# A gMLP mixer on 1024 tokens at a time: split weights shared by two blocks, a seven-product output projection, LN1 in two VectorE passes

## The chip, the core and the metric

One core of a Trainium2 chip runs the kernel alone. The metric is the device time of one execution in microseconds (us). TensorE multiplies matrices, VectorE and ScalarE do elementwise work, GpSimd does elementwise work out of SBUF, and SyncE issues every transfer of this kernel but two.

## The reference

The kernel computes one decoder layer for x of 2048 tokens by 1024 features, all in float32, with a conditioning vector c:

```python
sh1, sc1, g1, sh2, sc2, g2 = split(silu(c) @ mod_w + mod_b, 6)
h = x * (1 + sc1) + sh1
u, v = split(gelu(h @ w_in + b_in), 2)            # 1024 features each
v = layer_norm(v)                                 # gain and bias of the mixer
sv = tril(w_s) applied over chunks of 128 tokens, per group of 128 features, + b_s
y = (u * sv) @ w_out
x = layer_norm(2**0.25 * x + (1 + g1) * y) * ln1_g + ln1_b
h = x * (1 + sc2) + sh2
y = (silu(h @ w_g) * (h @ w_u)) @ w_d             # hidden width 2816
x = layer_norm(2**0.25 * x + (1 + g2) * y) * ln2_g + ln2_b
```

## The kernel before

Each float32 operand of a matmul is split into a high and a low part in fp32r: `parts` (L91) makes the high part by a cast on ScalarE (L94) and the rest by a subtraction on VectorE (L95). A product of two operands is three matmuls, high by high, high by low and low by high (`HL`, L103). A "unit" tile holds both parts of 128 by 512.

The mixer runs over four blocks b of 512 tokens, one after the other. For a block, `v_part` computes v token-major: eight feature slices d, for each of which x is scaled and split and a row of wv is loaded and split, then 24 matmuls of 128 by 512 into eight banks of PSUM. `us_part` computes u feature-major, eight tiles i of 24 matmuls, and the spatial tiles s, four float32 matmuls each. The product u times sv is split again into yT. `y_part` multiplies yT by wo, eight slices of 24 matmuls into eight banks. So wv, wu and wo are loaded and split once for each block, four times in all. The residual, LN1 and its statistics follow during the next block's v: multiply by g1 and add alpha x on VectorE (L380, L381), statistics on VectorE, the normalisation on ScalarE (L174), gain and bias on GpSimd (L386, L388; for the last block the bias on VectorE). `h2_part` transposes the rows on TensorE (L409), scales them and writes operands for the feed-forward part to DRAM ("hop"). The feed-forward part (`ffn_in`, tiles f_0 to f_10 for each half of the tokens, and `ffn_out`) uses seven products of half-sized blocks in place of eight; its input weights are combined on GpSimd (L86).

The modulation vectors are built on the way: `mod_col` loads 512 KB of mod_w and reduces it on VectorE (L124). `spread` writes such a vector to DRAM and loads it back for all partitions (L147, L149). `ahead(makers, depth)` makes an operand that many steps before it is used. A planner puts each engine's instructions into one order before the run: among those that it takes to be ready, the one that stands first in the program; each engine and SyncE's queue then keep to that order. Tiles of one tag share a fixed number of buffers: the first block's loads share 17 buffers of 512 KB (`first`), later weight loads share three (`raw`), split weights seven units (`w`).

Of the kernel before, what the change touches and what calls it, by code (L numbers as in the profile page):

```python
# [13 lines left out]
P = 128  # L14
D = 1024
# [22 lines left out]
def gmlp_swiglu_layer(  # L38
    ctx: ExitStack,
    tc: tile.TileContext,  # L40
    x, xT, c, modwT, modb,
# [78 lines left out]
    def mod_col(k, d, plus, tag="late"):  # L120
# [91 lines left out]
    def token_major(operands, nk, name, between=()):  # L212

        ps = [[bank(f"{name}_ps{t}{h}") for h in range(2)] for t in range(NT)]
        for k, (a, w) in enumerate(operands):
            for t in range(NT):
                for part, wpart in HL:
                    for h in range(2):
                        nc.tensor.matmul(  # L219
                            ps[t][h],  # L220
                            lhsT=a[:, part, t * P : (t + 1) * P],
                            rhs=w[h][:, wpart, :],
                            start=(k == 0 and part == 0 and wpart == 0),
                            stop=(k == nk - 1 and part == 1),
                        )
            for f in between[k :: nk]:
                f()
        return ps

    def feature_major(w, rhs, name):  # L230

        ps = bank(name)
        n = 0
        for d in range(ND):
            for wpart, part in HL:
                nc.tensor.matmul(  # L236
                    ps,
                    lhsT=w[d // 4][:, wpart, (d % 4) * P : (d % 4 + 1) * P],
                    rhs=rhs[d][:, part, :],
                    start=(n == 0),  # L240
                    stop=(n == 3 * ND - 1),
                )
                n += 1
        return ps

# [5 lines left out]
    def start():  # L251
        cact = new("cact", "cact")
# [32 lines left out]
    def v_operands(b, hT):  # L285
        def operands(d):
            if b == 0:
                sh1[d] = mod_col(0, d, 0.0, "first")
                sc1[d] = mod_col(1, d, 1.0, "first")
            r = new("xh" if b else "first", f"xT{b}_{d}", HALF)  # L290
            nc.sync.dma_start(out=r, in_=xT[d, :, b * TB : (b + 1) * TB])
            nc.vector.tensor_scalar(r, r, sc1[d], sh1[d], ALU.mult, ALU.add)
            hT.append(parts(r, f"hT{b}_{d}", "hT"))
            return hT[d], load_w(wv[d * P : (d + 1) * P, :], f"wv{b}_{d}", "raw" if b else "first")

        return ahead([lambda d=d: operands(d) for d in range(ND)])

    def v_part(b, operands, between):
        ps = token_major(operands, ND, f"v{b}", between)
        if b == 0:  # L300
            env["first"].close()
            env["mix"] = phase("left", yT=(8, UNIT), raw=(3, ROW), bcv=(3, ROW), vrow=(4, ROW))
            env["bv"] = bcast(bv, "bv_bc", "bcv")
        vh = [new("vrow", f"v{b}_{t}") for t in range(NT)]
        for t in range(NT):
            for h in range(2):
                sl = slice(h * 512, (h + 1) * 512)
                nc.vector.tensor_tensor(out=vh[t][:, sl], in0=ps[t][h], in1=env["bv"][:, sl], op=ALU.add)
            nc.scalar.activation(vh[t], vh[t], AF.Gelu)

        def norm(t):
            st = stats_tile(f"lnv{b}_{t}")
# [6 lines left out]
    def us_part(b, hT, vh, norm, between, mods):
        u = [None] * ND  # L320
        yT = [None] * ND

        weights = ahead([lambda i=i: load_w(wu[i], f"wu{b}_{i}") for i in range(ND)], 1)
        if b == 0:
            setup_spatial()

        def u_tile(i):
            w = next(weights)
            p = feature_major(w, hT, f"u{b}_{i}_ps")
            u[i] = new("u", f"u{b}_{i}")  # L330
            nc.scalar.activation(u[i], p, AF.Gelu, bias=colc[:, i : i + 1])

        def s_tile(i):
            p = bank(f"s{b}_{i}_ps")
# [14 lines left out]
            nc.vector.tensor_tensor(out=sv, in0=sv, in1=u[i], op=ALU.mult)  # L349
            yT[i] = parts(sv, f"yT{b}_{i}", "yT")  # L350

        for i, step in enumerate("u0 n0 u1 n1 u2 n2 n3 u3 h u4 s0 s1 u5 s2 s3 u6 s4 s5 s6 u7 s7".split()):
            if i < len(mods):
                mods[i]()
            if step == "h":
                between()
            else:
                {"u": u_tile, "n": norm, "s": s_tile}[step[0]](int(step[1]))
        return yT

    def y_part(b, yT, following, between):
        operands = ahead([lambda i=i: (yT[i], load_w(wo[i * P : (i + 1) * P, :], f"wo{b}_{i}")) for i in range(ND)])
        ps = token_major(operands, ND, f"y{b}", between)
        following()
        rows = [new("late", f"r{b}_{t}") for t in range(NT)]
        last = b == NB - 1
        for r, p in zip(rows, ps):
            for q, sl in enumerate((lo, hi)):
                if last:
                    nc.vector.tensor_tensor(out=r[:, sl], in0=p[q], in1=env["g1"][:, sl], op=ALU.mult)  # L370
                else:
                    nc.scalar.copy(out=r[:, sl], in_=p[q])

        def norm(t):
            r = rows[t]
            xt = new("h3" if last else "late", f"x{b}_{t}")
# [452 lines left out]
```

## Time and profile before

| what | value |
|---|---|
| median of 3 runs | 1888.29 us (1886.86 to 1888.87) |
| profiled execution, its own time | 1890.18 us |
| span of the trace of that execution | 1888.5 us |
| mean granted TensorE clock, as a share of full | 0.991 |
| TensorE busy, share of the span | 98% |
| VectorE, ScalarE, GpSimd busy | 68%, 39%, 32% |
| moved by DMA | 338.72 MB |

The span runs from the first to the last instruction; the execution's own time has 1.7 us around it. Matmuls are pipelined, so a busy TensorE has no idle time between instructions but need not be at its best; what it does without a pause is read from the spacing of matmuls. The mixer's stretch is from 0 to 606 us, where the first matmul of f_0 begins.

### The profile page before, as it was taken

The numbers are of one execution on the slowest core, as the hardware profiler recorded it, in microseconds if no ns is written. First come the engines' busy times: TensorE is split into PE (matmuls) and PEld (weight loads), VectorE is DVE, ScalarE is ACT, GpSimd is POOL, SyncE is SP. The second block draws the span as 40 slices with busy tenths as digits, with TensorE's granted clock in tenths as the row PEclk, the third lists the DMA queues.
The fourth block names the chain that finished last, engine by engine and source line by source line (L and its number), as shares of the span: only waits on it lengthen the run. The fifth ranks groups of instructions, "written<-read, shape, count | busy, mean of one in ns | idle before, by whom it ended". The sixth has DMA issues, their size and how long they took to land.

```text
span 1888.5 us, 23484 instructions
## 1 busy us (share of the span) xinstructions
PE 1844.8 (98%) x8264; PEld 1528.4 (81%) x8264; DVE 1278.1 (68%) x1901; ACT 736.3 (39%) x1216; POOL 595.1 (32%) x379
## 2 busy tenths in 40 slices
PE   7999999999999899999999999999999999999997
PEld 6887888878888788888887888888888888888886
DVE  8486965875856975567768856677666344455858
ACT  3433453453454444343335433333334333333320
POOL 0000500550502565665454644554453000000104
PEclk9899999999999999999999999999999999999999
DMA  9358545564435455445645435455545656556532
GB/s 354 126 199 279 195 151 205 191 232 166 136 144 184 173 178 176 143 162 190 205 168 192 141 119 173 151 173 196 199 157 189 217 185 195 185 162 194 172 118 100
DMA packets 149320, 338.72 MB, mean 179 GB/s; under 512 B 18225, under 2 KB 22353, under 8 KB 149202
## 3 DMA queue, kind: packets, MB, share of 16 engines
q1 hardware_dynamic: 149138, 337.19, 52.9%
q8 instruction: 64, 1.05, 0.2%
q14 instruction: 54, 0.44, 0.1%
q0 software_dynamic: 64, 0.03, 0.0%
HBM read 245.14 MB, written 92.02 MB: 179 GB/s over the span
## 4 chain that ended last, share of the span: by engine, by line
PE 85%; DVE 10%; DMA 3%; issue 1%; ACT 1%; SPq 0%; DVEq 0%; ACTq 0%
PE o L597 21%; PE u_ps L236 7%; PE y_ps L219 7%; PE v_ps L219 5%; DVE modw L124 2%; PE f_5u_X L455 1%; PE f_4u_X L455 1%; PE f_3u_X L455 1%; PE f_2u_X L455 1%; PE f_9g_X L455 1%; PE f_9u_X L455 1%; PE f_8u_X L455 1%; PE f_7u_X L455 1%; PE f_7g_X L455 1%; PE f_6u_X L455 1%; PE f_6g_X L455 1%
## 5 line engine op out<-in xcount | busy, mean ns | idle before, releaser
L597 PE MATMUL o<-wd_w,alw 128*128 128x512 f32 x1848 | 419.2, 389 | 0.0
L597 PEld LDWEIGHTS o<-wd_w,alw 128*128 128x128 f32 x1848 | 346.8, 188 | 72.0
L219 PE MATMUL v_ps<-wv,hT 128*128 128x512 f32 x768 | 180.5, 397 | 16.0 <-ACT wv L94 11.9
L219 PEld LDWEIGHTS v_ps<-wv,hT 128*128 128x128 f32 x768 | 147.5, 192 | 48.1 <-ACT wv L94 12.1
L236 PE MATMUL u_ps<-hT,wu 128*128 128x512 f32 x768 | 183.2, 398 | 0.8 <-ACT h L410 0.5
L219 PE MATMUL y_ps<-wo,yT 128*128 128x512 f32 x768 | 177.6, 393 | 4.2 <-DVE sv L342 4.2
L219 PEld LDWEIGHTS y_ps<-wo,yT 128*128 128x128 f32 x768 | 145.4, 190 | 34.8 <-issue 4.5
L236 PEld LDWEIGHTS u_ps<-hT,wu 128*128 128x128 f32 x768 | 145.9, 192 | 31.8 <-issue 1.0
L95 DVE TENSOR_TENSOR alw<-al,alw 128x512 fp32r<-128x512 f32 x154 | 100.5, 687 | 87.6 <-ACT alw L94 87.6
L94 ACT CAST alw<-al 128x512 fp32r<-128x512 f32 x154 | 89.0, 620 | 140.8 <-PE o L597 138.7
L188 POOL TENSOR_TENSOR ln_rss<-ln_ves,mhalf 128x4 f32<-128x4 f32 x3 | 7.4, 2467 | 378.2 <-DVE ln_ves L187 378.2
L162 POOL TENSOR_TENSOR ln_rs<-ln_ve,mhalf 128x1 f32<-128x1 f32 x20 | 19.4, 979 | 327.1 <-DVE ln_ve L160 316.8
L95 DVE TENSOR_TENSOR wd_w<-wdl,wd_w 128x512 fp32r<-128x512 f32 x77 | 53.0, 691 | 68.5 <-ACT wd_w L94 68.5
L95 DVE TENSOR_TENSOR wu<-wu_raw,wu 128x512 fp32r<-128x512 f32 x64 | 63.4, 1004 | 51.9 <-ACT wu L94 51.8
L94 ACT CAST wd_w<-wdl 128x512 fp32r<-128x512 f32 x77 | 47.7, 622 | 106.6 <-PE o L597 78.2
L94 ACT CAST wv<-wv_raw 128x512 fp32r<-128x512 f32 x64 | 37.5, 620 | 99.5 <-PE v_ps L219 44.6
L124 DVE SCALAR_TENSOR_TENSOR modw<-modw,cact 128x1024 f32<-128x1024 f32 x48 | 58.6, 1225 | 18.9 <-DMA modw<-in_modwT 18.9
L95 DVE TENSOR_TENSOR wv<-wv_raw,wv 128x512 fp32r<-128x512 f32 x64 | 47.8, 767 | 21.8 <-ACT wv L94 21.7
L95 DVE TENSOR_TENSOR wo<-wo_raw,wo 128x512 fp32r<-128x512 f32 x64 | 47.4, 749 | 21.2 <-ACT wo L94 21.2
L94 ACT CAST wo<-wo_raw 128x512 fp32r<-128x512 f32 x64 | 38.6, 616 | 44.2 <-PE y_ps L219 43.1
L94 ACT CAST wu<-wu_raw 128x512 fp32r<-128x512 f32 x64 | 38.3, 615 | 36.3 <-PE v_ps L219 19.2
L551 DVE TENSOR_TENSOR wd<-wd,g_bc 128x512 f32<-128x512 f32 x44 | 36.9, 861 | 12.7 <-DMA wd<-in_wd 12.3
(610 smaller groups left out, 3753.4 us busy)
## 6 DMA issues: line engine op xcount, KB each, us to landing
al<-aop SPq DMA_DIRECT2D x154, 256.0 KB, 2.8
modw<-in_modwT SPq DMA_DIRECT2D x48, 512.0 KB, 8.3
aop<-aop_s SPq DMA_DIRECT2D x88, 256.0 KB, 2.0
wv_raw<-in_wv SPq DMA_DIRECT2D x32, 512.0 KB, 4.7
wu_raw<-in_wu SPq DMA_DIRECT2D x32, 512.0 KB, 4.1
wo_raw<-in_wo SPq DMA_DIRECT2D x32, 512.0 KB, 3.5
wd<-in_wd SPq DMA_DIRECT2D x44, 256.0 KB, 4.1
wdT<-wd SPq DMA_DIRECT2D x44, 256.0 KB, 4.1
```

Of the source, the lines that this page charges most:

```text
L94: nc.scalar.copy(out=o[:, 0, :], in_=src)
L95: nc.vector.tensor_tensor(out=o[:, 1, :], in0=src, in1=o[:, 0, :].bitcast(F32), op=ALU.subtract)
L124: nc.vector.scalar_tensor_tensor(out=w, in0=w, scalar=1.0, in1=env["cact"], op0=ALU.mult, op1=ALU.mult, accum_out=modc[:, j : j + 1],)
L162: nc.gpsimd.tensor_tensor(out=rs, in0=ve, in1=mhalf, op=ALU.pow)
L188: nc.gpsimd.tensor_tensor(out=rs, in0=ve, in1=mhalf.broadcast_to([P, m]), op=ALU.pow)
L219: nc.tensor.matmul(ps[t][h], lhsT=a[:, part, t * P : (t + 1) * P], rhs=w[h][:, wpart, :], start=(k == 0 and part == 0 and wpart == 0), sto ...
L236: nc.tensor.matmul(ps, lhsT=w[d // 4][:, wpart, (d % 4) * P : (d % 4 + 1) * P], rhs=rhs[d][:, part, :], start=(n == 0), stop=(n == 3 * ND ...
L455: nc.tensor.matmul(ps, lhsT=w[:, wpart, k * P : (k + 1) * P], rhs=a[k][:, part, :], start=(first and k == 0 and wpart == 0 and part == 0), ...
L551: nc.vector.tensor_tensor(out=b, in0=b, in1=env["g2"][:, cs], op=ALU.mult)
L597: nc.tensor.matmul(ps[:, cs], lhsT=a[:, part, p * P : (p + 1) * P], rhs=w[:, wpart, cs], start=(first and part == 0 and wpart == 0), stop= ...
```

## The change

The mixer runs over two pairs of blocks, 1024 tokens each, in a function `mixer(sb, jobs, u_done)` that replaces `v_part`, `us_part` and `y_part`; `load_w`, `token_major` and `feature_major` go.

- v: two passes y over its 512-column halves. In the first, x for 1024 tokens is loaded, scaled on ScalarE and split into 2 units for each slice; wv is loaded by halves and split once for the pair. u: each split tile of wu serves both blocks.
- y: u times sv stays in float32 as A. Products 1, 2, 6, 5, 7, 3, 4 of four slices each take sums of A made on VectorE and split on the way (`left_y`), and operands of wo that are loaded already split from DRAM (`right_y`).
- `wo_prep(k)`, four times in the first pair during u: loads two rows of wo, multiplies by g1, makes seven operands, splits each and stores both parts to DRAM, 512 KB each.
- LN1: alpha x is added as a bank is read; gain and bias are two `scalar_tensor_tensor` passes over 1024 columns on VectorE; nothing of it is on GpSimd but one small power for four rows. The first block's runs after product 3, the second's (`norm(1)`) in the next v or in f_0.
- The loads of x and of the raw weights share three buffers (`xs`), split weights six units (`w`). Rows of x1 are loaded back from DRAM for the transposes of all four blocks (before: of the last); two blocks' transposes lie in the second pair's u, two in ffn_in. Preparation of wd starts at f_7 (before: f_6).

```diff
+    def wo_prep(k):
...
+        def store(n, src):
+            nc.sync.dma_start(out=wot[n][k], in_=parts(src, f"wo{n}_{k}", "w").bitcast(F32))
+        def scale(q):
+            nc.vector.tensor_tensor(out=w[q], in0=w[q], in1=env["g1"], op=ALU.mult)
+            for n, cs in ((("B11", lo),), (("B21", lo), ("B22", hi)))[q]:
+                store(n, w[q][:, cs])
+        def totals():
+            b11, b12, b21, b22 = w[0][:, lo], w[0][:, hi], w[1][:, lo], w[1][:, hi]
+            for n, o, a, b in (("T1", b11, b12, b11), ("T3", b12, b22, b12), ("T2", b22, b22, b11), ("T4", b21, b21, b22)):
+                nc.vector.tensor_tensor(out=o, in0=a, in1=b, op=ALU.subtract)
+                store(n, o)
...
+    def mixer(sb, jobs, u_done):
...
+            r = new("xs", f"xT{sb}_{d}")
+            nc.sync.dma_start(out=r, in_=xT[d, :, sb * D : (sb + 1) * D])
+            nc.scalar.activation(r, r, AF.Identity, bias=sh1[d], scale=sc1[d])
+            for x, cs in enumerate((lo, hi)):
+                h[x][d] = parts(r[:, cs], f"h{blocks[x]}_{d}", ("hA", "hB")[x])
...
+            for k in range(ND):
+                w = next(made)
+                for x in range(2):
+                    for t in range(NT):
+                        for part, wpart in HL:
+                            nc.tensor.matmul(
+                                ps[x][t], lhsT=h[x][k][:, part, t * P : (t + 1) * P], rhs=w[:, wpart, :],
...
+        for i in range(ND):
+            w = next(made)
+            for x in range(2):
+                u_tile(x, i, w)
+            also("u", i)
...
+        def left_y(pr, k):
+            a11, a12, a21, a22 = (A[x, y, k] for x in range(2) for y in range(2))
+            t = s1[k // 2][:, (k % 2) * 512 : (k % 2 + 1) * 512]
+            if pr == 6:
+                for o, a, b, op in ((t, a21, a22, ALU.add), (a21, a11, a21, ALU.subtract), (a11, t, a11, ALU.subtract), (a12, a12, a11, ALU.subtract)):
+                    nc.vector.tensor_tensor(out=o, in0=a, in1=b, op=op)
+            return parts({1: a11, 2: a12, 6: a11, 5: t, 7: a21, 3: a12, 4: a22}[pr], f"y{sb}_S{pr}{k}", "hB")
...
+        def evacuate(pr, j, ps):
+            if pr in (1, 6, 7, 4):
+                x, y = {1: (0, 0), 6: (0, 1), 7: (1, 1), 4: (1, 0)}[pr]
+                with_x(x, j, (lo, hi)[y], ps[j])
+            if pr in (2, 3):
+                o = rows[0][j][:, (lo, hi)[pr == 3]]
+                add(o, ps[j], o)
+            if pr == 7:
+                o = rows[1][j][:, hi]
+                add(o, z[j], o)
+            for p, x, y in ((2, 0, 0), (3, 0, 1), (7, 1, 1), (4, 1, 0)):
+                if p == pr:
+                    bn(rows[x][j], sts[x][j], y)
+        def norm(x):
+            for t, (mu, rs, nm) in enumerate(norms_of(sts[x], f"ln1_{blocks[x]}")):
+                r = rows[x][t]
+                nc.vector.scalar_tensor_tensor(out=r, in0=r, scalar=mu, in1=env["ln1g"], op0=ALU.subtract, op1=ALU.mult)
+                nc.vector.scalar_tensor_tensor(out=r, in0=r, scalar=rs, in1=env["ln1b"], op0=ALU.mult, op1=ALU.add)
+                nc.sync.dma_start(out=x1d[blocks[x]][t * P : (t + 1) * P, :], in_=r)
...
+            for k in range(NK):
+                a, w = next(made)
+                for j in range(4):
+                    for part, wpart in HL:
+                        nc.tensor.matmul(
+                            ps[j], lhsT=a[:, part, j * P : (j + 1) * P], rhs=w[:, wpart, :],
...
+            for j in range(4):
+                evacuate(pr, j, ps)
+            if pr == 3:
+                norm(0)
+        return lambda: norm(1)
...
-    late = phase("left", late=(12, ROW))
-    mix = phase("left", w=(7, UNIT), cact=(1, ROW))
-    env["first"] = phase("left", first=(17, ROW))
-    early = phase("right", hT=(8, UNIT), u=(5, HALF), xh=(2, HALF), sv=(2, HALF))
+    late = phase("left", lc=(2, ROW), late=(10, ROW))
+    mix = phase("left", hB=(8, UNIT), u=(16, HALF), w=(6, UNIT), xs=(3, ROW), lt=(3, ROW))
+    early = phase("right", hA=(8, UNIT), sv=(2, HALF), bc=(4, ROW))
...
+    for k in range(NK):
+        jobs["u", k + 1] = [wo_prep(k)]
...
+    norm = mixer(0, jobs, lambda: None)
+    jobs = {("v", 0, 0): [norm]}
```

## Rows read from the trace of the kernel before

**Rows 1.** The page, part 1: busy time, share of the span, instructions.
```profile
PE 1844.8 (98%) x8264; PEld 1528.4 (81%) x8264; DVE 1278.1 (68%) x1901; ACT 736.3 (39%) x1216; POOL 595.1 (32%) x379
```

**Rows 2.** The page, part 5: TensorE's groups of the mixer.
```profile
L219 PE MATMUL v_ps<-wv,hT 128*128 128x512 f32 x768 | 180.5, 397 | 16.0 <-ACT wv L94 11.9
...
L236 PE MATMUL u_ps<-hT,wu 128*128 128x512 f32 x768 | 183.2, 398 | 0.8 <-ACT h L410 0.5
L219 PE MATMUL y_ps<-wo,yT 128*128 128x512 f32 x768 | 177.6, 393 | 4.2 <-DVE sv L342 4.2
```

**Rows 3.** Chain that ended last: start us, us, engine, tile, line, count.
```profile
465.08 43.52 PE v_ps L219 x192
...
272.19 0.89 PE s_ps L337 x8
```

**Rows 4.** Timeline of TensorE: start us, us, instruction, count, idle before it.
```profile
11.86 46.34 PE L219 MATMUL v_ps<-wv,hT 128*128 128x512 f32 x192 [11.86 <-ACT wv L94]
...
163.14 1.07 PE L219 MATMUL v_ps<-wv,hT 128*128 128x512 f32 x4
...
179.06 34.96 PE L219 MATMUL v_ps<-wv,hT 128*128 128x512 f32 x142 [3.90 <-DVE wv L95]
213.86 21.93 PE L236 MATMUL u_ps<-hT,wu 128*128 128x512 f32 x96
...
272.83 43.78 PE L219 MATMUL y_ps<-wo,yT 128*128 128x512 f32 x192
...
360.35 22.03 PE L236 MATMUL u_ps<-hT,wu 128*128 128x512 f32 x96 [0.22 <-DVE v L308]
...
414.59 3.27 PE L219 MATMUL y_ps<-wo,yT 128*128 128x512 f32 x13
422.05 43.03 PE L219 MATMUL y_ps<-wo,yT 128*128 128x512 f32 x179 [4.19 <-DVE sv L342]
...
645.82 0.73 PE L455 MATMUL f_1g_Y<-h2A,f_1g_w 128*128 128x512 f32 x2 [1.30 <-ACT f_1g_w L94]
647.45 2.57 PE L455 MATMUL f_1g_Y<-h2A,f_1g_w 128*128 128x512 f32 x10 [0.90 <-DVE f_1g_w L95]
...
653.53 2.58 PE L455 MATMUL f_1u_Y<-h2A,f_1u_w 128*128 128x512 f32 x10 [3.06 <-DVE f_1u_w L95]
```

**Rows 5.** SyncE's waits from 0 to 720 us: total, times, longest.
```profile
SPq L149 <- DMA g_bc_line<-modc: 17.9, 2, 9.2
```

**Rows 6.** Groups of VectorE and ScalarE by shape, 0 to 612 us.
```profile
L292 DVE TENSOR_SCALAR xT<-xT,modc 128x512 f32<-128x512 f32 x32 | 17.3, 547 | 13.6 <-DMA xT<-in_xT 13.0
...
L381 DVE SCALAR_TENSOR_TENSOR r<-x,r 128x1024 f32<-128x1024 f32 x12 | 14.5, 1222 | 0.0
...
L94 ACT CAST hT<-xT 128x512 fp32r<-128x512 f32 x32 | 19.4, 620 | 21.6 <-DVE xT L292 21.3
...
L174 ACT ACTIVATE r<-r,ln_nm,ln_rs 128x1024 f32<-128x1024 f32 x12 | 14.1, 1234 | 3.4 <-DVE ln_nm L173 3.4
```

**Rows 7.** The chain again, VectorE back to back in block 1.
```profile
164.51 2.29 DVE modw L124 x4
...
180.64 1.80 DVE wv L95 x3
```

**Rows 8.** Timeline of VectorE with GpSimd busy, two stretches.
```profile
411.48 1.77 DVE L95 TENSOR_TENSOR wo<-wo_raw,wo 128x512 fp32r<-128x512 f32 x1
...
647.32 3.41 DVE L388 TENSOR_TENSOR r<-r,ln1b_bc 128x1024 f32<-128x1024 f32 x1
```

**Rows 9.** The page, part 5: the power of four columns on GpSimd.
```profile
L188 POOL TENSOR_TENSOR ln_rss<-ln_ves,mhalf 128x4 f32<-128x4 f32 x3 | 7.4, 2467 | 378.2 <-DVE ln_ves L187 378.2
```

**Rows 10.** Windows: busy of each engine (count), granted clock, DMA share, GB/s.
```profile
20.00:40.00 20.00, 20.00 (x90) 16.57 (x89) 19.85 (x43) 7.09 (x13) 0.00 (x0) 1.00 1.03 413
...
160.00:180.00 20.00, 15.87 (x67) 12.55 (x66) 18.05 (x34) 6.76 (x13) 0.00 (x0) 0.94 1.03 419
```

**Rows 11.** DMA issues: count, KB each, median us from issue to landing.
```profile
x1d<-r SPq DMA_DIRECT2D x16, 512.0 KB, 4.9
```

More of the change, by code (lines that the diff above doesn't have):

```diff
@@ L210, in ahead @@
         return results()
[L212 to L244, printed above, removed]
     x1d = [dram.tile([TB, D], F32, name=f"x1d{b}") for b in range(NB)]
@@ L283, in setup_spatial @@
         env["wm"], env["tb"] = wm, tb
[L285 to L312, printed above, removed]
-            for q in range(2):
-                bn(vh[t], st, q)
-            normalise(vh[t], st, f"lnv{b}_{t}")
-        return vh, norm
@@ L319, in us_part @@
[L319 to L334, printed above, removed]
+    wot = {n: [dram.tile([P, 2, 512], F32, name=f"wo{n}_{k}") for k in range(NK)] for n in B_OF.values()}
@@ L348, in s_tile @@
             )
[L349 to L376, printed above, removed]
-            row = b * TB + t * P
-            nc.sync.dma_start(out=xt, in_=x[row : row + P, :])
-            if not last:
-                nc.vector.tensor_tensor(out=r, in0=r, in1=env["g1"], op=ALU.mult)
-            nc.vector.scalar_tensor_tensor(out=r, in0=xt, scalar=ALPHA, in1=r, op0=ALU.mult, op1=ALU.add)
-            st = stats_tile(f"ln1_{b}_{t}")
-            for q in range(2):
-                bn(r, st, q)
-            normalise(r, st, f"ln1_{b}_{t}")
-            nc.gpsimd.tensor_tensor(out=r, in0=r, in1=env["ln1g"], op=ALU.mult)
-            e = nc.vector if last else nc.gpsimd
-            e.tensor_tensor(out=r, in0=r, in1=env["ln1b"], op=ALU.add)
-            nc.sync.dma_start(out=x1d[b][t * P : (t + 1) * P, :], in_=r)
-        return rows, norm
@@ new lines, in s_tile @@
+            nc.vector.tensor_tensor(out=u[x, i], in0=sv, in1=u[x, i], op=ALU.mult)
+        made = ahead([lambda i=i: wu_pieces(i) for i in range(ND)], 1)
+        norm_v(0)
+        norm_v(1)
+        spatial = {3: (0, 1), 4: (2,), 5: (3, 4), 6: (5,), 7: (6, 7)}
+        for i in range(ND):
+            w = next(made)
+            for x in range(2):
+                u_tile(x, i, w)
+            also("u", i)
+            for f in spatial.get(i, ()):
+                for x in range(2):
+                    s_tile(x, f)
@@ new lines, in right_y, with with_x @@
+        def right_y(pr, k):
+            w = new("w", f"y{sb}_T{pr}{k}")
+            nc.sync.dma_start(out=w.bitcast(F32), in_=wot[B_OF[pr]][k])
+            return w
+        rows = [[new("late", f"r{b}_{t}") for t in range(NT)] for b in blocks]
+        sts = [[stats_tile(f"ln1_{b}_{t}") for t in range(NT)] for b in blocks]
+        def with_x(x, t, cs, ps):
+            xt = new("lt", f"x{blocks[x]}_{t}{cs.start}", HALF)
+            row = blocks[x] * TB + t * P
+            nc.sync.dma_start(out=xt, in_=inp_x[row : row + P, cs])
+            nc.vector.scalar_tensor_tensor(out=rows[x][t][:, cs], in0=xt, scalar=ALPHA, in1=ps, op0=ALU.mult, op1=ALU.add)
```

183 lines of the change are left out of this document (121 added, 62 removed).

## Prediction

> **What bounds the kernel now.** I read the page's busy shares first: TensorE is busy for 98% of the span, VectorE for 68% [rows 1]. The groups of the mixer come next: v, u and y have 768 matmuls of 128 by 512 each [rows 2]. A mean of 390 to 398 ns there is the life of one pipelined matmul; what one costs is its spacing, and the chain shows that: 192 of them follow each other in 43.52 us, 0.2267 us each, and a pair of spatial accumulations, one s tile, takes 0.89 us [rows 3]. So a stage without a pause is priced by its count, and what a block takes beyond that is waiting.
>
> The timeline of TensorE then says where it waits [rows 4]. The first matmul starts at 11.86 us. Block 0's v needs 46.34 us (2.8 over). Block 1's v lasts from 163.14 to 213.86, 50.7 us, 7.2 over: 3.90 us of it is a wait for VectorE's part of wv, and the 142 matmuls behind that wait take 34.96 us instead of 32.2, since the granted clock fell. Block 1's u and s last 59.0 us (213.86 to 272.83), block 2's only 54.2 (360.35 to 414.59), so 4.8 over. Block 2's y lasts from 414.59 to 465.08, 50.5 us, 7.0 over, with a wait of 4.19 us for its last operand. In f_1 three waits of 1.30, 0.90 and 3.06 us make 5.3. Blocks 2 and 3 have v and y stages without any loss. So TensorE sets the end, and the mixer's losses are hand-overs at which VectorE's queue is behind.
>
> **What the change removes from TensorE.** v and u keep 768 matmuls each. y falls from 768 to 2 pairs x 7 products x 4 slices x 4 tiles x 3 = 672. That is 96 x 0.2267 = 21.8 us, on the engine that sets the end. Spatial tiles and transposes keep their number; two blocks' transposes move to ffn_in, which changes no sum.
>
> **What else it removes.** Block 1's loss of 7.2 us in v had its cause in the queue: SyncE waited 9.2 us at a time for the round trip of the g1 vector [rows 5], the loads of the next vectors and of wv stood behind it, and VectorE then took the vectors first. In the new order that round trip falls into the first pair's u, where several operands are made ahead: -7.2. The wait for the last operand of y in block 2 came from a product u times sv that had to be made and split after the last s tile; products 1 and 2 now take the first four slices: -7.0. The extra of block 1's u goes for the larger part: -3.3 of 4.8, as transposes remain. The 5.3 us in f_1 I drop here and count its successor below. Together -22.8.
>
> **What it adds, in order of time.**
> The start. The first slice of x has 1024 columns and goes through ScalarE, 1.23 us where VectorE took 0.55 for 512, and one more cast of 0.62 stands before that of wv [rows 6]: +1.3.
>
> Block pair 0's first v pass has the same bytes as block 0's v, but x and wv have 3 buffers in place of a share of 17. A slice of x holds its buffer until VectorE has split both halves, so the second piece of wv is requested at about 13.4 us and stands behind ten loads of mod_w that found buffers. These and what is before them are some 7.4 MB, 19 to 20 us at the 413 GB/s of a full window [rows 10]; the second piece is ready near 21.4 us where TensorE wants it at 18.7. +2.7 (0 if those loads wait, 12 if more go ahead).
>
> wo_prep in u of pair 0. Back to back, a subtraction of 512 columns takes VectorE 0.60 us and a pass over 1024 columns 1.14 [rows 7]. One wo_prep is two passes and eleven operations of 512, 8.9 us; four are 35.5. In the same four steps of u (4 x 10.9, with six s tiles 48.9 us) VectorE splits wu (4.8) and reads the s tiles (7.6): 47.9 of 48.9, full, but one step of wu is always made ahead. The DMA carries 4 x (1.05 + 3.67 + 0.52) = 21 MB, 50.5 us at the 413 to 419 GB/s of the two fullest windows [rows 10]. That is 1.6 over, I take +2 (0 to 25, below).
>
> The y stages. Of 76.2 us (336 x 0.2267) VectorE needs 88 operations x 0.60 = 53 and one LN1 of about 10: 63, so it keeps pace on the whole. Behind product 7 it reads two banks and makes statistics for each tile before product 3 may write into z: the fourth is released 4.6 us after product 7 where TensorE wants it at 2.0. Other tiles can go first. +1.25 each (0 to 2.6): +2.5.
>
> The end of y in pair 0, to v. This is the weak place. After product 3 VectorE reads four banks (free at 2.8 us), makes LN1's small numbers with a power on GpSimd of 2.5 us [rows 9], at 6.6, and then does eight passes of 1.14, to 15.7. Product 4 lasts 48 x 0.2267 = 10.9, so its banks are read from 5.4 us after its end, one every 1.2 us. TensorE meanwhile can do the first block's half of the pieces that are split (2.7 us each, into the four banks of z). Two pieces are, made in VectorE's spare time in products 5 and 3, and cover just this. Then norm(1) takes VectorE for another 13 us, of which 2.5 are free for one more piece; the fifth piece is split 26.2 us after y, wanted at 22.4. +3.8, and with a clock loss as after the 3.90 us wait [rows 4], 3 us, it is +7 (0 to 15). Queued behind norm(1) on VectorE are the splits of v's pieces; TensorE waits for those.
>
> The end of y in pair 1, to f_0. The same queue, but now S1 and the weights of f_0 stand behind it: the third product of f_0 starts 2 to 3 us late, and the weights of its fourth, emitted after norm(1), come about 5 late. +8 (0 to 16), in the place of f_1's 5.3.
>
> LN1 itself costs nothing more on VectorE than the multiply and the add it replaces, two passes of 1.22 us then and now [rows 6]. Its time is covered where y and v give VectorE spare time; where the cover is gone its price is in the last two terms. The reloading of rows of x1 and the later preparation of wd cost nothing: they have tens of us until used.
>
> Added: 1.3 + 2.7 + 2 + 2.5 + 7 + 8 = 23.5. The sum: -21.8 - 22.8 + 23.5 = -21.1. Against the profiled execution's own 1890.18 us that is 1869.1; the median of the runs is 1.9 lower, so I forecast 1867 us: the matmuls' saving, with old waits exchanged for new ones.
>
> **A rule weighed against a row.** Beside GpSimd a split of 512 columns took 1.77 us and a pass of 1024 columns 3.41 [rows 8], against 0.60 and 1.14 without. Moving LN1's passes off GpSimd takes this away from the mixer, and I counted it in the waits that go. But norm(1) of pair 1 falls into f_0, where GpSimd combines weights. If each of its eight passes met it, it would last 8 x 2.2 = 17.5 us longer. The Trainium skill (SBUF — State Buffer, "Who interferes with whom") says that an instruction of VectorE with two SBUF inputs contends with one of GpSimd that reads SBUF, and that the later one is blocked for the whole instruction. By that rule the new passes, which have two SBUF inputs each, are as exposed as the additions were, and the trace agrees for those with 3.41 us.
>
> **The rivals.**
> 1. Both hand-overs and the y stages are hidden: VectorE's spare time reaches for more pieces than I count, or TensorE finds other tiles. Speaking for it: blocks 2 and 3 have no loss in v although LN1 lies there. 1867 - 17.5 = 1849.
> 2. The hand-overs cost their full price: TensorE waits until the last bank is read (9.7 us) and for norm(1) (13) less two pieces (10.9), with a clock loss 15 in each place: 1867 + 15 = 1882. For it: block 1's v, where vectors and residual passes starved the split of wv in just this way.
> 3. norm(1) in f_0 meets GpSimd in every pass: 1867 + 17.5 = 1884, no difference. Against it: GpSimd is not always busy there.
> 4. Slower: wo_prep starves u. Its 28 splits go through the six units of `w`, of which wu holds four; a split holds its unit for a cast, a subtraction and a store of 512 KB, 0.62 + 0.69 + 4.9 [rows 6, 11] = 6.2 us. Through two units that is 87 us, where 48.9 and one step ahead of 10.9 are there: 27 us of waiting in place of my 2, 1892. It decides from 23 us of waiting, that is at 5.9 us for each split. Against it: a finished step of u gives two more units, and the median store of 4.9 us holds queueing.
> That the count does not fall is no case: the loops of y are written out in the diff.
>
> **Chances.** The forecast 0.50 (its own range 1857 to 1877), rival 1 0.13, rival 2 0.15, rival 3 0.05, rival 4 0.15, the rest, between 2 and 4, 0.02. A measurement of this kernel tells about 0.2% from no change, 3.8 us. Faster takes the forecast, rival 1, and most of 2, a little of 3: 0.75. Same: 0.08. Slower: rival 4 and a little of the rest: 0.17. The range of 8 in 10 goes from rival 1's 1849 to 1889, which leaves out most of rival 4 and the outer tail of rival 1.
>
> **What the profile after would show.** 672 matmuls in y, and y stages of 76 to 79 us. The first matmul near 13.2 us and the first pass of v ending near 60. In pair 0's u, waits of TensorE for wu of 2 us or less; 20 or more would be rival 4. Behind y of both pairs, VectorE in the two LN1 passes while TensorE waits for its splits or banks. No waits like those of block 1's v and block 2's y. Wrong I would be if the planner put norm's passes after the splits (rival 1), or if stores of wo held up the loads of wu.

## Result and the profile after

The change made the kernel slower: 1945.66 us median of 4 runs (1944.42 to 1947.14) against 1887.78 (4 runs), a ratio of 1.0307 (1.0289 to 1.0325). The forecast was 1867 us, faster. The profiled execution spans 1943.9 us, 55.4 more than before.

The page's parts 1 and 5 after the change, to be held against [rows 1, 2]:

```profile
PE 1839.9 (95%) x8168; PEld 1518.1 (78%) x8168; DVE 1231.7 (63%) x1785; ACT 685.3 (35%) x1116; POOL 508.4 (26%) x327
...
L449 PE MATMUL y<-y_T,y_S 128*128 128x512 f32 x672 | 156.7, 395 | 30.6 <-ACT y_S L94 26.3
```

The 96 matmuls are gone, and every engine has less to do. But TensorE, busy 98% before, is busy 95%: the time went into waiting. The timeline of TensorE, to be read as [rows 4], says where:

```profile
12.10 7.20 PE L313 MATMUL v_ps<-wv,h 128*128 128x512 f32 x24 [12.10 <-ACT h L94]
32.03 7.47 PE L313 MATMUL v_ps<-wv,h 128*128 128x512 f32 x24 [12.74 <-ACT wv L94]
41.42 12.80 PE L313 MATMUL v_ps<-wv,h 128*128 128x512 f32 x48 [1.91 <-ACT wv L94]
55.41 11.18 PE L313 MATMUL v_ps<-wv,h 128*128 128x512 f32 x48 [1.19 <-ACT wv L94]
69.60 56.28 PE L313 MATMUL v_ps<-wv,h 128*128 128x512 f32 x240 [3.01 <-ACT wv L94]
125.72 0.62 PE L347 MATMUL u_ps<-h,wu 128*128 128x512 f32 x2
...
318.27 46.00 PE L313 MATMUL v_ps<-wv,h 128*128 128x512 f32 x202
368.26 44.06 PE L313 MATMUL v_ps<-wv,h 128*128 128x512 f32 x182 [4.00 <-DVE v L83]
...
524.79 22.03 PE L449 MATMUL y<-y_T,y_S 128*128 128x512 f32 x96
573.13 35.43 PE L449 MATMUL y<-y_T,y_S 128*128 128x512 f32 x144 [26.31 <-ACT y_S L94]
610.38 22.04 PE L449 MATMUL y<-y_T,y_S 128*128 128x512 f32 x96 [1.81 <-DVE r L83]
633.13 0.73 PE L522 MATMUL f_0g_X<-h2A,f_0g_w 128*128 128x512 f32 x2 [0.71 <-ACT f_0g_w L94]
639.51 4.14 PE L522 MATMUL f_0g_X<-h2A,f_0g_w 128*128 128x512 f32 x10 [4.09 <-DVE f_0g_w L95]
659.73 1.65 PE L522 MATMUL f_0g_Z<-h2S,f_0g_w 128*128 128x512 f32 x3 [6.06 <-DVE h2S L95]
```

Three places hold the loss: v of the first pair, 113.6 us where its 384 matmuls need 87.05; one wait of 26.31 us in y of the second pair; and f_0. By stages of the two timelines:

| stretch | before | after | difference |
|---|---|---|---|
| first matmul | 11.86 | 12.10 | +0.2 |
| v of all blocks | 184.5 | 207.5 | +23.0 |
| u, s and transposes | 228.9 | 225.7 | -3.2 |
| y of all blocks | 181.2 | 187.8 | +6.6 |
| f_0 and f_1 | 74.2 | 96.4 | +22.2 |
| the rest | | | +6.6 |

The rest is the stretch from f_2 to the end. It holds 24 of the 32 transposes of the one block whose transposes moved to ffn_in (ffn_in has 64 now, 32 before; eight take 0.79 us), a longer wait in f_10 (4.88 us, 3.16 before), and a lower clock behind that wait (the next 12 matmuls took 5.23 us, 3.04 before).

**What SyncE did in the first v.** Its timeline (start, us, transfer, count; transfers are issued in this order):

```profile
5.17 9.73 SPq L118 DMA_DIRECT2D modw<-in_modwT  x8
15.74 0.33 SPq L136 DMA_DIRECT2D bv_bc<-in_bv  x1
16.98 2.87 SPq L118 DMA_DIRECT2D modw<-in_modwT  x3
20.73 0.33 SPq L224 DMA_DIRECT2D wm<-in_ws  x1
22.02 0.33 SPq L296 DMA_DIRECT2D wv_raw<-in_wv  x1
23.27 0.33 SPq L136 DMA_DIRECT2D ln1g_bc<-in_ln1g  x1
24.51 0.33 SPq L136 DMA_DIRECT2D ln1b_bc<-in_ln1b  x1
...
54.30 0.39 SPq L142 DMA_DIRECT2D g_bc_line<-modc  x1
```

The second piece of wv is asked for at 22.02 us, behind eleven vectors of mod_w, bv and wm; ln1g and ln1b, first used at 305.5 us, go ahead of the third. At 54.30 comes the g1 row, 1024 numbers stored four bytes at a time. The windows of the two stretches:

```profile
12.00:40.00 28.00, 14.67 (x48) 11.25 (x48) 24.32 (x52) 5.97 (x9) 1.68 (x1) 0.76 1.03 417
40.00:70.00 30.00, 24.38 (x98) 19.31 (x99) 17.18 (x36) 12.24 (x17) 0.00 (x0) 0.94 0.87 241
```

In the first the DMA engines are full at 417 GB/s, and TensorE, busy for half of it, is granted a mean clock of 0.76. In the second they are busy for 0.87 of the time and move only 241 GB/s.

**What VectorE did in the second y and in f_0.** Its timeline:

```profile
541.70 0.69 DVE L410 SCALAR_TENSOR_TENSOR r<-x,y 128x512 f32<-128x512 f32 x1 [1.95 <-DMA x<-in_x]
...
564.46 0.69 DVE L410 SCALAR_TENSOR_TENSOR r<-x,y 128x512 f32<-128x512 f32 x1 [10.17 <-DMA x<-in_x]
565.06 2.49 DVE L394 TENSOR_TENSOR s<-u,u 128x512 f32<-128x512 f32 x4
...
631.60 4.86 DVE L430 SCALAR_TENSOR_TENSOR r<-r,ln_rss,ln1b_bc 128x1024 f32<-128x1024 f32 x4
...
638.77 0.68 DVE L95 TENSOR_TENSOR f_0g_w<-f_0g_b,f_0g_w 128x512 fp32r<-128x512 f32 x1
...
650.60 2.31 DVE L429 SCALAR_TENSOR_TENSOR r<-r,ln_mvs,ln1g_bc 128x1024 f32<-128x1024 f32 x1
...
669.42 4.87 DVE L430 SCALAR_TENSOR_TENSOR r<-r,ln_rss,ln1b_bc 128x1024 f32<-128x1024 f32 x4
```

The last bank of product 1 is read only at 564.46 (L410), after a wait for its x; the sums from which product 6's operands are split (L394) stand behind it. ScalarE's casts stand late too, so the first candidates were two: ScalarE's order, or transfers that land late. The transfers issued from 547 to 556 us (count, KB each, median us to landing) take this long:

```profile
y_T<-woT SPq DMA_DIRECT2D x3, 512.0 KB, 15.0
...
x<-in_x SPq DMA_DIRECT2D x2, 256.0 KB, 13.7
...
g_bc_line<-modc SPq DMA_DIRECT2D x1, 4.0 KB, 15.8
```

### The profile page after: what moved, and what is told of

It is laid out like the page before. It is cut to its first block, busy times and chain, and to the rows that moved or that the text cites. A ratio compares the mean times of both kernels' runs of the same rounds, so it can differ in the third digit from the quotient of the medians.

```text
span 1943.9 us, 23188 instructions
## 1 busy us (share of the span) xinstructions
PE 1839.9 (95%) x8168; PEld 1518.1 (78%) x8168; DVE 1231.7 (63%) x1785; ACT 685.3 (35%) x1116; POOL 508.4 (26%) x327
## 4 chain that ended last, share of the span: by engine, by line
PE 63%; issue 6%; DVE 3%; DMA 2%; POOL 1%; SPq 0%; ACT 0%; DVEq 0%; POOLq 0%
PE o L664 20%; PE f_4g_X L522 1%; PE f_2g_X L522 1%; PE f_5g_X L522 1%; PE f_3g_X L522 1%; PE f_4u_X L522 1%; PE f_3u_X L522 1%; PE f_2u_X L522 1%; PE f_5u_X L522 1%; PE f_1u_X L522 1%; PE f_9u_X L522 1%; PE f_9g_X L522 1%; PE f_8u_X L522 1%; PE f_8g_X L522 1%; PE f_7u_X L522 1%
## 5 line engine op out<-in xcount | busy, mean ns | idle before, releaser
L313 PE MATMUL v_ps<-wv,h 128*128 128x512 f32 x768 | 185.0, 404 | 34.9 <-ACT wv L94 18.9
L313 PEld LDWEIGHTS v_ps<-wv,h 128*128 128x128 f32 x768 | 150.2, 196 | 69.2 <-ACT wv L94 20.5
L449 PE MATMUL y<-y_T,y_S 128*128 128x512 f32 x672 | 156.7, 395 | 30.6 <-ACT y_S L94 26.3
L347 PE MATMUL u_ps<-h,wu 128*128 128x512 f32 x768 | 180.3, 394 | 1.4 <-ACT wu L94 1.4
L449 PEld LDWEIGHTS y<-y_T,y_S 128*128 128x128 f32 x672 | 127.4, 190 | 59.1 <-ACT y_S L94 27.0
L347 PEld LDWEIGHTS u_ps<-h,wu 128*128 128x128 f32 x768 | 144.4, 190 | 31.5 <-ACT wu L94 1.8
L94 ACT CAST wd_w<-wdl 128x512 fp32r<-128x512 f32 x77 | 47.8, 623 | 106.5 <-PE o L664 79.5
L95 DVE TENSOR_TENSOR wu<-wu_raw,wu 128x512 fp32r<-128x512 f32 x32 | 21.7, 686 | 63.0 <-ACT wu L94 63.0
L94 ACT CAST y_S<-u 128x512 fp32r<-128x512 f32 x48 | 29.6, 622 | 76.5 <-PE y L449 44.9
L95 DVE TENSOR_TENSOR y_S<-u,y_S 128x512 fp32r<-128x512 f32 x48 | 37.1, 791 | 20.5 <-ACT y_S L94 20.4
L352 ACT ACTIVATE u<-u_ps,colc 128x512 f32<-128x512 f32 x32 | 22.0, 686 | 73.2 <-PE u_ps L347 73.2
L94 ACT CAST wv<-wv_raw 128x512 fp32r<-128x512 f32 x32 | 19.8, 619 | 71.3 <-DMA wv_raw<-in_wv 36.2
L410 DVE SCALAR_TENSOR_TENSOR r<-x,y 128x512 f32<-128x512 f32 x32 | 21.5, 681 | 29.2 <-DMA x<-in_x 18.1
```

The lines of the kernel that those rows point to most:

```text
L94: nc.scalar.copy(out=o[:, 0, :], in_=src)
L95: nc.vector.tensor_tensor(out=o[:, 1, :], in0=src, in1=o[:, 0, :].bitcast(F32), op=ALU.subtract)
L313: nc.tensor.matmul(ps[x][t], lhsT=h[x][k][:, part, t * P : (t + 1) * P], rhs=w[:, wpart, :], start=(k == 0 and part == 0 and wpart == 0), ...
L347: nc.tensor.matmul(p, lhsT=w[d // 4][:, wpart, (d % 4) * P : (d % 4 + 1) * P], rhs=h[x][d][:, part, :], start=(d == 0 and wpart == 0 and p ...
L352: nc.scalar.activation(u[x, i], p, AF.Gelu, bias=colc[:, i : i + 1])
L410: nc.vector.scalar_tensor_tensor(out=rows[x][t][:, cs], in0=xt, scalar=ALPHA, in1=ps, op0=ALU.mult, op1=ALU.add)
```

## Experiments

All ratios are to the kernel before, run beside it (medians of 1887.8 to 1891.5 us). The stretches, in us, are read from the TensorE timeline of one execution of each: the first v from its first matmul to u, the second y from its first matmul to f_0's, and f_0 with f_1 up to f_2.

| run | median us | ratio (95%) | first v | second y | f_0, f_1 |
|---|---|---|---|---|---|
| the change | 1945.66 | 1.0307 (1.0289-1.0325) | 113.6 | 108.3 | 96.4 |
| e1 | 1926.76 | 1.0196 (1.0166-1.0225) | 107.3 | 99.1 | 97.7 |
| e2 | 1943.15 | 1.0282 (1.0234-1.033) | 112.1 | 102.7 | 94.6 |
| e3 | 1928.82 | 1.0206 (1.016-1.0253) | 104.4 | 105.6 | 96.7 |
| e4 | 1928.10 | 1.0203 (1.0173-1.0232) | 97.5 | 107.4 | 97.0 |
| e5 | 1944.66 | 1.029 (1.0237-1.0344) | 113.3 | 108.8 | 95.9 |
| e6 | 1928.22 | 1.0203 (1.0155-1.0252) | 106.9 | 99.2 | 97.2 |
| e7 | 1946.16 | 1.0298 (1.0232-1.0365) | 113.0 | 108.5 | 102.5 |
| e8 | 1927.18 | 1.0198 (1.0149-1.0247) | 113.5 | 107.5 | 83.7 |
| e9 | 1927.31 | 1.019 (1.0151-1.0229) | 113.7 | 96.3 | 90.0 |
| e10 | 1901.83 | 1.0063 (1.004-1.0086) | 108.1 | 84.3 | 85.1 |
| e11 | 1939.79 | 1.0256 (1.0224-1.0288) | 111.5 | 108.4 | 93.1 |
| e12 | 1891.04 | 1.0002 (0.9989-1.0015) | 97.6 | 83.8 | 84.1 |
| e13 | 1889.26 | 0.9993 (0.9982-1.0004) | 96.2 | 82.5 | 87.8 |
| e14 | 1890.18 | 1.0000 (0.9991-1.0010) | 98.2 | 87.2 | 80.4 |
| e15 | 1895.05 | 1.0037 (1.0024-1.0049) | 94.8 | 80.3 | 93.9 |

**The first v: buffers, early loads, the scattered row.** e3 gives the raw wv of pair 0 buffers of its own:

```diff
-            r = new("xs", f"wv{sb}_{y}{k}_raw", HALF)
+            r = new("xs" if sb else "u", f"wv{sb}_{y}{k}_raw", HALF)
```

> Edit: in the first pair wv's pieces are loaded into the 16 buffers of u, which are free then, so that x alone has the three buffers. Theory B (three buffers for x and wv starve the first pass of v): the first pass of v, 57.5 us from the first matmul to the eighth piece's ready point, falls to 46 or less, and the time by 11 to 20 us, to 1926 to 1935. Theory E (loads not needed yet, which have free buffers of their own, go ahead and fill the DMA): the bytes in front stay, and the time falls by less than 5 us.

e4 lets GpSimd write one column of the late tiles (bv, wm, the row vectors, wo, the vectors of g1) out of a late slice of h, so that they can't be loaded before:

```diff
+    def gate(t, d):
+        g = env["h0"][d]
+        nc.gpsimd.tensor_copy(out=t[:, 0:1], in_=g[:, 0, 0:1].bitcast(F32))
...
```

> Edit: the loads of bv, of the spatial weights, of LN1's rows, of wo and of mod_w for g1 first have one column of their buffer written from a late piece of h, so that they can't be issued before it is there. Theory E: the first pass has some 15 MB in front of its last piece and not 22; it falls from 57.5 us to 46 or less, and the time by 11 to 20 us, to 1926 to 1935. Theory B: the pieces of x and wv still wait for buffers, and the time falls by less than 5 us.

e1 turns the modulation row on TensorE and stores eight rows of 512 bytes:

```diff
-        nc.sync.dma_start(out=line.rearrange("d p -> p d"), in_=modc[:, k * ND : (k + 1) * ND])
+        ps = bank(f"{name}_ps")
+        nc.tensor.transpose(ps[0:ND, 0:P], modc[:, k * ND : (k + 1) * ND], ident)
...
+        nc.scalar.copy(out=lt[0:ND, :], in_=ps[0:ND, 0:P])
+        nc.sync.dma_start(out=line, in_=lt[0:ND, :])
```

> Edit: the vectors g1 and g2 go to DRAM as eight rows of 512 bytes, transposed on TensorE first, where the changed kernel stores 1024 elements of 4 bytes each. Theory L (the scattered store of g2, issued in product 1 of the second pair's y, holds up every transfer behind it for some 15 us): the wait of 26.3 us before product 6 falls below 6, its clock loss goes too, and the time falls by 25 to 35 us, to 1911 to 1921. Theory C (ScalarE's casts of A11 and A12 stand ahead of those of y's operands and wait for their own loads): the wait stays above 15 us and the time falls by less than 12.

Measured in the first v: e3 -9.2 us, e4 -16.1, e1 -6.3. That stretch lasts 26.5 us longer than its 384 matmuls need. Holding back the loads that nobody waits for yet takes off most of it. Own buffers take off a third: the waits for wv go, and two for slices of x come in their place (5.90 and 5.70 us). The parts overlap. e4 also moves the store of the g1 row, to 78.2 us, and e12, which is e4 with e1 and more, is no shorter (97.6); with the loads held back, own buffers are worth 1.4 us more (e13 against e12). So the loads are the larger cause, and the three shared buffers make it worse. e4's timeline of TensorE has one long wait left:

```profile
25.85 9.06 PE L326 MATMUL v_ps<-wv,h 128*128 128x512 f32 x32 [6.43 <-ACT wv L94]
35.19 74.64 PE L326 MATMUL v_ps<-wv,h 128*128 128x512 f32 x328 [0.28 <-DVE wv L95]
```

e1 also took 9.2 us out of the second y, whose wait fell from 26.31 to 18.90 us; theory L below had promised less than 6. Its edit changes two things at once, the form of the store and its time (behind the transpose the g1 row goes at 137.9 us in place of 54.3, the g2 row at 901.2 in place of 547.5); what each is worth isn't separated. In pieces of 4 bytes the two rows took 10.7 and 15.8 us to land, 10.0 and 9.7 before the change. For rows of 512 bytes the trace gives no landing, but the load that waits for the g1 row was issued 3.3 us after its store in e12 and 3.9 us after it in e1.

**The second y: whose order is it?** Theory C: ScalarE and VectorE, which take their work in order, hold y's operands behind the splits of f_0's A11 and A12. Theory L: the scattered row delays all transfers behind it. e2 asked for the loads of A11 and A12 after the second mixer in the program:

> Edit: the loads and splits of A11 and A12 for f_0 are emitted after the second pair's y, not before it. Theory C: the wait of 26.3 us before product 6 falls below 6; f_0 starts up to 10 us later; the time falls by 16 to 26 us, to 1920 to 1930. Theory L: the loads of x and of wo's operands behind the scattered store are as late as before; a wait of 10 to 20 us stays, and what f_0 loses makes the time 1935 to 1955.

They were issued in the second y all the same (A11 from 532.7 to 545.0 us, A12 from 552.6), so it says little about C. e5 holds them by data: a column of their buffers is written from the first operand of product 3 of that y.

```diff
...
+                if sb == 0 and n in ("A11", "A12"):
+                    nc.gpsimd.tensor_copy(out=t[:, 0:1], in_=env["y_S3"][:, 0, 0:1].bitcast(F32))
```

> The buffers into which A11 and A12 of pair 0 are read back are first written by a one-column GpSimd copy that reads the first operand of product 3 of the second y, so their reads and splits can't stand ahead of that y's operands. The scattered store of g2 stays. Theory C (ScalarE and VectorE take their work in order, and the operands of product 5 stand behind the splits of A11 and A12, which wait 9 and 17 us for their reads): the 26.3 us wait in the second y falls below 8 us, the kernel by 15 to 26 us from 1945.7, to 1920 to 1931; less by up to 10 us if f_0 then starts late. Theory L (the scattered store delays every transfer behind it, whichever operand it is): the wait stays above 18 us, the time within 6 us of 1945.7.

> The edit before together with the modulation row written through a TensorE transpose in eight rows of 512 bytes, which by itself gave 1926.8 us with a wait of 18.9 us in the second y. If C and L are two halves of one wait: under 5 us of it are left, 1900 to 1916 us. If C alone is the cause: the same wait as with C alone, and a time lower than that by only the 6 us that the transposed row gave in the first v and up to 8 us elsewhere. If the wait is the DMA engines' sheer load there: above 12 us left, over 1918 us.

The A casts were gone from the stretch and a wait of 22.86 us stayed; e6, which is e5 with e1's edit, was no better than e1. C is refuted. But e5's timelines of VectorE and ScalarE show the next suspect, which the A casts had hidden:

```profile
556.64 0.69 DVE L413 SCALAR_TENSOR_TENSOR r<-x,y 128x512 f32<-128x512 f32 x1 [17.59 <-DMA x<-in_x]
...
562.01 2.49 DVE L394 TENSOR_TENSOR s<-u,u 128x512 f32<-128x512 f32 x4
```

```profile
568.81 2.43 ACT L94 CAST y_S<-u 128x512 fp32r<-128x512 f32 x4 [40.16 <-DVE u L394]
```

VectorE stands at a bank read, waiting 17.59 us for x, with the sums behind it. Theory X: x shares its three buffers with the vectors and the rows of x1, is asked for too late, and then lands late. e9 gives it the raw rows of wu:

```diff
-            xt = new("lt", f"x{blocks[x]}_{t}{cs.start}", HALF)
+            if sb and t % 2 == 0:
+                env["xp"] = new("xs", f"x{blocks[x]}_{t}{cs.start}", ROW)
+            xt = env["xp"][:, t % 2 * 512 : t % 2 * 512 + 512] if sb else new("lt", ...)
```

> x for the banks of blocks 2 and 3 goes, two halves to a row, into the three row buffers of the u weights' raw rows, which are free by then, in place of the three that it shares with the modulation weights and the rows for the transposes; the x of product 1 can then be loaded before the second y. Nothing else changes, the scattered store stays. Theory X (VectorE's bank reads of product 1 stand ahead of the sums for product 6 and 5, and wait 10 to 18 us for x): the 26.3 us wait before product 5 of the second y falls below 10 us, 1922 to 1934 us. Theory L (the scattered store or the load on the DMA engines, whatever is behind it): it moves to y's stored operands or to ScalarE's casts and stays above 18 us, within 6 us of 1945.7.

> The same together with the modulation row written through a transpose. Theory X with nothing behind it: the second y without a wait above 4 us, and 18 to 24 us less than the 1926.8 us of the transposed row alone has left there: 1906 to 1914 us. If X is not the cause: 1921 to 1931 us, as with the transposed row alone.

X holds. In e9 the four bank reads run without a pause and the sums follow, 17 us into that y where it was 40; TensorE waits 7.3 us in three places:

```profile
536.52 2.47 DVE L412 SCALAR_TENSOR_TENSOR r<-x,y 128x512 f32<-128x512 f32 x4
538.91 2.48 DVE L394 TENSOR_TENSOR s<-u,u 128x512 f32<-128x512 f32 x4
```

```profile
545.77 2.09 PE L451 MATMUL y<-y_T,y_S 128*128 128x512 f32 x8 [1.70 <-DMA y_T<-woT]
...
557.37 29.09 PE L451 MATMUL y<-y_T,y_S 128*128 128x512 f32 x120 [4.73 <-DMA y_T<-woT]
```

The longest is L's: a wait for y's stored operands, with the scattered row issued at 545.65 here. Without the row, in e10, no wait inside that y is over 1.01 us. e10 took 43.8 us off, e1 18.9 and e9 18.4. The surplus over their sum, 6.5 us, is smaller than the intervals of these ratios are wide, so it isn't shown that the two are worth more together.

**f_0: VectorE, and GpSimd in its place.** Theory V: VectorE, with LN1 of the pair in its queue, sets the end of f_0. e7 makes LN1 of the pair as before (`sb` is the pair), e8 leaves its passes out:

```diff
+                if sb:
+                    nc.scalar.activation(r, r, AF.Identity, bias=nm, scale=rs)
+                    nc.gpsimd.tensor_tensor(out=r, in0=r, in1=env["ln1g"], op=ALU.mult)
+                    nc.gpsimd.tensor_tensor(out=r, in0=r, in1=env["ln1b"], op=ALU.add)
```

> LN1 of blocks 2 and 3 in the form of the kernel before: one ScalarE pass and two GpSimd passes, 16 GpSimd passes at the 2.65 us of [rows 8]'s kind, 42 us in all; 16 VectorE passes of 1.2 to 2.3 us go, 22 us in all. Theory V (VectorE sets the end in the first 45 us of f_0, where PE waits some 20 us): the waits fall by 8 to 16 us, the time to 1929 to 1938. Theory G (GpSimd then holds up the differences of f_0's weights): the waits of f_0 don't fall or move to GpSimd, 1941 to 1960. Theory K (late loads are the cause): within 4 us of 1945.7.

> Leaves out the two LN1 passes of blocks 2 and 3 (their rows go on without scale and shift), so 22 us of VectorE work are gone from the end of the second y and from f_0, and nothing takes their place. Theory V: f_0's waits fall from about 20 us to under 8, the time to 1925 to 1936. Theory K: within 4 us of 1945.7, the waits the same, on the splits of f_0's operands that come late.

Without the passes f_0 and f_1 take 12.7 us less: V holds for more than half of their loss. On GpSimd they take 6.1 us more than on VectorE, with new waits of 9.03 and 7.29 us for splits of f_0's weights, whose differences GpSimd makes. So GpSimd, where LN1's gain and bias were before, is no better place for them in f_0.

> The LN1 passes of block 2 are issued behind product 6 of f_0 and those of block 3 behind product 6 of f_1, the transposes of both one column block later; no work is left out. Theory V (the end of f_0 is set by VectorE, of whose work 22 us were LN1's; without them 1927.2 us): the waits of f_0 fall from about 20 to under 10 us, 1926 to 1938 us; what a later column block loses with VectorE that busy is at most the 3.2 us by which f_10 waits. Rival: VectorE is short in f_1 and f_2 as well, the wait moves there whole, within 4 us of 1945.7.

e11 puts the passes behind product 6 of f_0 and of f_1 in the program, and the transposes of both blocks one column block later. It hardly moved the passes: the second ones (L430) start from 630.7 to 671.4 us, 631.6 to 673.0 without the edit. By the code they can't go later, as S3, A22 and half of S4 go into the ten buffers of `late` that LN1's rows hold; that is argued, not shown. Its 5.9 us less are unexplained.

**Together.** e12 is e1, e4, e9 and e11's edit; e13 is e1, e4, e9 and own buffers for the first half of wv; e14 is e1, e4 and e9 with e8's omission; e15 is e13 with two of the eight row tiles of LN1 in e7's form.

> x early, the modulation row through a transpose, the late loads of the first pass held back and LN1 of blocks 2 and 3 later, all four together. If the four are the parts of the loss and don't share their time: first v -16, second y -22, f_0 -10, of 1945.7: 1893 to 1902 us, near the 1888 of the kernel before. If they are one shortage that moves on: over 1912 us.

> x early, the modulation row through a transpose, the late loads of the first pass held back, and the raw rows of the first half of wv in buffers of their own (the u tiles', free until then); LN1 stays where the change put it. The first v then has neither cause of its waits: if the 6.0 us that were left of them were the wait for a raw row's buffer, v ends 4 to 6 us sooner than with the late loads held back alone, 1884 to 1889 us against 1891; if they are the load of the first 8 MB itself, no change, 1890 to 1893 us.

> The three mends without the last one (wv's raw rows as the change has them), and the LN1 passes of blocks 2 and 3 left out (their rows go on unscaled). If VectorE, with LN1's 16 passes in it, is what is left in f_0, the waits of f_0 (some 14 us with the mends) fall below 5 us and the time to 1874 to 1881 us. If f_0 waits for its operands' reads instead, 1886 to 1892 us.

> As the own raw rows, and LN1 of the last two row tiles of block 3 in the form of the kernel before (one ScalarE and two GpSimd passes): 4 VectorE passes of 1.27 us less, 4 GpSimd passes of about 2.65 us more. If VectorE alone is short in f_0: 3 to 6 us less than with the own raw rows. If GpSimd, which makes the differences of f_0's weights, is as short: the same within 2 us, or up to 5 us more.

e12's TensorE line of the page, and its timeline at the same three places:

```profile
PE 1829.5 (97%) x8170; PEld 1512.2 (80%) x8170; DVE 1229.7 (65%) x1785; ACT 684.0 (36%) x1118; POOL 513.9 (27%) x348
```

```profile
25.94 83.95 PE L330 MATMUL v_ps<-wv,h 128*128 128x512 f32 x360 [6.01 <-ACT wv L94]
...
564.50 22.01 PE L468 MATMUL y<-y_T,y_S 128*128 128x512 f32 x96 [0.59 <-issue]
590.53 1.22 PE L541 MATMUL f_0g_X<-h2A,f_0g_w 128*128 128x512 f32 x2 [4.03 <-ACT f_0g_w L94]
...
611.21 4.63 PE L541 MATMUL f_0g_Z<-h2S,f_0g_w 128*128 128x512 f32 x10 [5.67 <-DVE f_0g_w L95]
```

Buffers, the order of transfers and the form of one store give back 54.6 us, nearly the whole loss, with the arithmetic of the change untouched. y of the pair now takes 79.7 us (506.76 to 586.5), and the mixer ends 19.8 us sooner than before. The wait of 4.03 us ahead of f_0 takes back a part of it, f_0 and f_1 another 9.9, and what follows 5.5. Owned rows for wv shortened the first v by 1.4 us: the wait for wv is gone, and one of 4.04 us for a slice of x is left. That this is the first loads themselves is argued, not shown. In e14 LN1's absence saved 3.7 us in f_0 and f_1 against e12, and 7.4 against e13, where LN1 stands as the change has it. The second y lost 3.4 and 4.7 us to waits for y_T (one of 4.05), so the time stayed the same; why y_T came later there is open. In e15 it cost 6.1 us in f_0 and f_1 to share the passes with GpSimd. None of the versions beats the kernel before by more than can be told apart.

## Why the prediction was wrong

Against the sum, the first v costs 21.0 us more than forecast (26.5 over its matmuls, not 5.5), the second y 30.9 (108.3, not 76.2 and 1.25), f_0 and f_1 19.5 (22.2 over before, not 2.7) and what follows 6.6. That is nearly all of the 76.5 us between 1869.1 and the profiled execution's own 1945.6.

**The count was right.** There are 672 matmuls, y of pair 0 takes 79.5 us (forecast 76 to 79), with a wait of 1.71 us behind product 7 (1.25). The first matmul starts at 12.10 (13.2), and u of pair 0 has one wait of 1.36 us for wu (2 or less; rival 4 is refuted). In e12 the two y stages take 78.5 and 79.7 us, 23.0 less than the 181.2 of before, so the saving of 21.8 is there.

**"+7 (0 to 15)" at the end of y in pair 0: the number came by luck.** The v behind it lasts 6.9 us over its matmuls, but its first 202 matmuls follow y without a pause. The forecast wait for pieces of wv did not come; rival 1 had this place right. TensorE waits 4.00 us at 364.3, between the two passes of v, for banks that VectorE reads only behind norm(1)'s last passes:

```profile
362.75 4.86 DVE L430 SCALAR_TENSOR_TENSOR r<-r,ln_rss,ln1b_bc 128x1024 f32<-128x1024 f32 x4
367.53 1.87 DVE L83 TENSOR_TENSOR v<-v_ps,bv_bc 128x512 f32<-128x512 f32 x3
```

The granted clock, 0.68 on average from 364 to 372 us and 0.90 from there to 380, makes the rest. So the queue of VectorE was named rightly, and the place and the operand wrongly.

**"In the new order that round trip falls into the first pair's u": false.** The store of g1 goes at 54.30 us, in the middle of v, as soon as its columns are there. I read the time of a transfer from its place in the program; here it went when its buffer and its data were there. The row's cost moved from block 1's v into the first v, where e1 measures 6.3 us for it: what -7.2 took away came back inside the 26.5 us of the next point.

**"+2.7 (0 if those loads wait, 12 if more go ahead)": mis-sized.** v of pair 0 lasts 26.5 us over its matmuls; with the 2.8 of before it was to be 5.5. I priced one piece of wv, requested at 13.4 us, behind ten loads. It was requested at 22.02, with eleven vectors, bv and wm before it, more before the third piece, and the scattered row behind that. e4 measures 16.1 us for the loads that went ahead and for the row; the clock of 0.76 is part of the bill. My upper bound of 12 left out loads that I had counted as u's.

**The second y had no term.** I priced y's stages by VectorE's busy time (63 of 76 us) and by operands, and took x as present. The 26.31 us came from x: three shared buffers, a late request, a landing of 13.7 us with the scattered row in the queue, and a VectorE that keeps to its order, so that a wait for 256 KB held the operands of all products behind the second (e9, e10). Theory C, my first reading of the profile after, fell too: the casts that stood in ScalarE's queue were late themselves, not the cause.

**"+8, in the place of f_1's 5.3": mis-sized, by the mechanism named.** VectorE's queue at the end of the second y is the place, but f_0 and f_1 take 22.2 us more than before, where 2.7 more were forecast. e8 puts 12.7 us on LN1, and e10 11.3 on x and the row; the two overlap. That x and the row act here through late bank reads ahead of f_0's splits is argued, not shown.

**The rule on VectorE and GpSimd.** Of norm(1)'s eight passes in f_0 only the two beside GpSimd's work of 650.1 to 657.9 us lasted 2.3 us, the others 1.2 to 1.3: rival 3's 17.5 us were 2.1. The other half of that choice, which I had not weighed, was e7's: with GpSimd making f_0's differences, the passes cost more there.

**"Two blocks' transposes move to ffn_in, which changes no sum".** One block's did: 96 of these matmuls lay in the mixer before and 64 do now. Its 3.4 us are what u lost (-3.2), so little is left of the -3.3 for block 1's u. "The reloading of rows of x1 ... cost nothing" fails too: the transposes in the second pair's u wait five times for x1c, 2.9 us in all.

## To carry to other kernels

In this kernel a load went out when its buffer was free, not where it stands in the program. For each load that the first stage needs, list what has free buffers ahead of it, and for each small operand (a residual tile, a row vector) ask which pool it waits for and what stands behind its reader on an engine that works in order. A stage whose end is set by transfers or by one engine's queue doesn't get faster by having fewer matmuls; here buffers and transfers decided over 54 us, the saving was 22. When a wait names a cast, follow it to the first instruction that waits for a transfer, hold that one back alone, and look again.

## Unexpected of the hardware

A store of 4 KB in pieces of 4 bytes lasted 15.8 us, and transfers of 256 and 512 KB issued around it took 13.7 to 15.0. The windows of the kernel after show the DMA engines busy and nearly idle in bytes at once (the last two columns are share and GB/s):

```profile
552.00:557.00 5.00, 0.00 (x0) 0.00 (x0) 2.29 (x4) 0.00 (x0) 0.00 (x0) 0.50 1.34 201
557.00:562.00 5.00, 0.00 (x0) 0.00 (x0) 0.00 (x0) 0.00 (x0) 0.00 (x0) 0.50 0.92 80
```

In e10, which has no such store there, the same stretch of y keeps its rate, and the operands of wo (y_T) land in 7.6 us:

```profile
540.00:545.00 5.00, 3.75 (x14) 2.55 (x15) 5.00 (x10) 5.00 (x10) 0.00 (x0) 1.00 1.04 411
545.00:550.00 5.00, 4.83 (x21) 3.65 (x21) 5.00 (x9) 0.69 (x2) 0.00 (x0) 1.00 1.03 417
550.00:555.00 5.00, 5.00 (x24) 4.15 (x23) 5.00 (x9) 2.28 (x4) 0.00 (x0) 1.00 1.03 413
```

In e9, which differs from e10 by that store alone, the rate falls as after the change, to 41 GB/s at the lowest. So one row of 4 KB held up the transfers around it. e10 takes the row out of this stretch as well as changing its form, so it does not show what a row of 512-byte pieces would do at the same place. The Trainium skill (DMA: Bandwidth & Descriptors, Specifications) gives 512 bytes as the least transfer for full rate. The runs agree for the row itself: 10.7 and 15.8 us in pieces of 4 bytes, at most 3.9 for the g1 row in pieces of 512.
